# The lowest score level of a gated linear recurrence, from window products to folded dot products

## The chip, the cores and the metric

One NeuronCore of a Trainium2 chip runs the whole program. The metric is device time in microseconds; the time of a kernel is the median of several executions. The engines named below are TensorE (PE; PEld is its weight load), VectorE (DVE), ScalarE (ACT), GpSimd (POOL) and SyncE (SP, which only issues DMAs here).

## The reference

A trunk of two residual layers over 512 tokens of width 2048, all in float32. The first, mixer A, is a gated linear recurrence (HGRN2) with 16 heads of 128 features; the second, mixer B, is softmax attention with forget gates. What matters here is mixer A's score matrix. For each head, with q and k of shape (512, 128) and g the log of the forget gate,

```python
b = jnp.cumsum(gc, axis=-2)
diff = b[..., :, None, :] - b[..., None, :, :]
decay = jnp.exp(jnp.where(mask, diff, -jnp.inf))
A = jnp.einsum('bhtd,bhsd,bhtsd->bhts', qc, kc, decay)
```

so a score A[t, s], s <= t, is the sum over the 128 features of q[t] k[s] times the product of the forget gates between s and t, and the output is A v, then a norm by head, a SiLU gate and the output projection.

## The kernel before

**Data.** Everything lies transposed: 128 features on the partitions, the 512 tokens along the free axis (T = 512, P = 128), in four windows of 128 tokens (NW = 4). Products are made in float32r with each factor split into a high and a low part: `split(src, h, l)` (L443) casts on ScalarE (L444) and takes the difference on VectorE (L445), and a product is three matmuls, high by high, high by low, low by high. `sum_parts` (L332) sums over the 128 partitions in another way: VectorE adds the upper 64 partitions to the lower 64 (L337), the sum's high part is cast into the lower half of a tile (L338) and its low part written to the upper half (L339), and one matmul with the constant matrix `ones` sums all 128 rows and puts the sum on every row (L340).

**Groups and tasks.** The projections run in groups (`group`, L220): 16 k-steps of twelve 512-column matmuls (L238 to L244), with the weights loaded by DMA and split just ahead (three buffers each of `wh` and `wl`). Mixer A has 16 groups in a hand-written order, `order_a` (q0 v0 q1 q2 v1 q3 g0 ...). After each k-step `pump` (L91) advances the waiting heads' generators by `RATE_A` = 2 steps, so the heads' work is placed between the matmuls of the groups. A head's generator is `mix_a` (L610); each `yield` in it ends a step. With this order as its starting point, the framework plans the order of instructions on each engine from the costs and due times that it assumes for them.

**A head in mixer A.** The scores are built by levels into the tile `at` (128 source tokens on the partitions, by window and query token). The lowest level covers blocks of four tokens: query and key 0 to 3 tokens apart (d = 0, 1, 2, 3) in the same block. `e` holds the gates' products over 1, 2, 3 and 4 tokens. Before, the level splits k (`k_split`), makes `pr`, q times the gates for d = 1 to 3 (L632), splits q and `pr` into `mh` and `ml` (two windows at a time), and for each window multiplies k's 128 tokens by 320 columns (`win_scores`, L592 to L594); of this product only the few diagonals are wanted, which four `put_scores` for each window pick with masks (a predicated copy, L587). Then q and k are scaled by the gates (L644, L649) for the next level. Two more levels (m = 4, 16), a level of 64-token halves (copied into `at` at L733) and products between windows (with scalings at L747) follow; at last `at` is split window by window into `ah` and `al` (L760, with offsets `AOFF` = 0, 512, 1024, 896) and multiplied by v in `attend` (L429).

The functions as they were before the change:

## Time and profile before

| | |
|---|---|
| median of 3 runs | 2010.18 us (2009.14 to 2012.45) |
| the profiled execution's own time | 2011.1 us |
| its span in the trace | 2009.4 us, mean granted TensorE clock 0.995 |
| TensorE, weight loads | 1978.4 us (98%), 1695.3 us (84%) |
| VectorE, ScalarE, GpSimd | 1558.7 us (78%), 1130.1 us (56%), 207.3 us (10%) |
| mixer A's stretch | 0 to about 878 us of the span |
| HBM | 184.73 MB read, 96 GB/s over the span with the writes |

A row of a group of instructions reads: line, engine, operation, output<-inputs by the program's names, partitions x elements, count | busy time in us, mean ns of one | idle time of the engine before them, and what ended it. A matmul's duration contains its latency; what one costs in a stream is the distance from its start to the next one's. A row of a wait reads: who <- for whom, us in total, times, longest. A row of a window reads: the stretch and its length, busy time of PE, PEld, DVE, ACT and POOL, granted clock, DMA share, GB/s.

### The profile page before, as it was taken

The page shows a single profiled execution, that of the slowest core. Times are in us where ns is not written, and L with a number is a line of the kernel's source. Part 1 is how long each engine was busy: PE and PEld are TensorE (multiplying, and loading weights), DVE is VectorE, ACT ScalarE, POOL GpSimd, SP SyncE. Part 2 cuts the span into 40 slices and gives each one's busy share as a digit, 9 for nine tenths or more (in the row PEclk, how much of TensorE's full clock was granted, in tenths as well). Part 3 has the DMA queues.
Part 4 walks back from the last instruction along what each step waited for, and adds up shares of the span by engine and source line. Part 5 has one row for each costly group of instructions (what it writes and reads, how often), then busy time and mean ns, then how long its engine had stood idle before and what let it go on. Part 6 is the DMA issues. An engine that isn't in the chain of part 4 may idle for free.

```text
span 2009.4 us, 28900 instructions
## 1 busy us (share of the span) xinstructions
PE 1978.4 (98%) x10218; PEld 1695.3 (84%) x10218; DVE 1558.7 (78%) x3321; ACT 1130.1 (56%) x2311; POOL 207.3 (10%) x365
## 2 busy tenths in 40 slices
PE   9999999999999999989999999999999999999898
PEld 7888888888888888879987888888888888888898
DVE  7969987979798889797893677776766676687877
ACT  6646655657566466653464555665555556576332
POOL 3303110203122030010000000000000000000100
PEclk9999999999999999999999999999999999999999
DMA  5222222222222222243432222322223332323443
GB/s 190 74 88 81 74 84 74 84 78 80 83 76 74 74 84 84 84 155 120 157 118 95 95 87 87 95 90 94 85 89 90 94 95 90 90 84 106 137 157 105
DMA packets 57600, 195.01 MB, mean 97 GB/s; under 512 B 7904, under 2 KB 8032, under 8 KB 57456
## 3 DMA queue, kind: packets, MB, share of 16 engines
q1 hardware_dynamic: 52192, 176.39, 28.0%
q0 software_dynamic: 5120, 16.78, 2.5%
q8 instruction: 80, 1.31, 0.3%
q14 instruction: 64, 0.52, 0.1%
q10 hardware_dynamic: 144, 0.01, 0.0%
HBM read 184.73 MB, written 8.42 MB: 96 GB/s over the span
## 4 chain that ended last, share of the span: by engine, by line
PE 83%; DVE 7%; DMA 5%; issue 3%; ACT 1%; POOL 1%; SPq 0%; POOLq 0%; DVEq 0%; ACTq 0%
PE gm L244 17%; PE gm L242 17%; PE gm L243 17%; PE gm L238 6%; PE gm L240 6%; PE gm L239 6%; DMA wr<-in_wa_q 3%; DVE w7l L445 2%; PE mx L594 2%; PE mx L593 2%; PE mx L592 1%; DMA wr<-in_wb_q 1%; PE mx L439 1%; PE mx L440 1%; PE mx L438 1%
## 5 line engine op out<-in xcount | busy, mean ns | idle before, releaser
L242 PE MATMUL gm<-xh,wh 128*128 128x512 f32 x1664 | 650.5, 392 | 0.1
L243 PE MATMUL gm<-xl,wh 128*128 128x512 f32 x1664 | 650.2, 391 | 0.0
L244 PE MATMUL gm<-xh,wl 128*128 128x512 f32 x1664 | 610.8, 392 | 0.2 <-DVE wl L445 0.2
L243 PEld LDWEIGHTS gm<-xl,wh 128*128 128x128 f32 x1664 | 313.2, 188 | 62.8
L242 PEld LDWEIGHTS gm<-xh,wh 128*128 128x128 f32 x1664 | 313.3, 188 | 62.6 <-DVE z L390 0.3
L244 PEld LDWEIGHTS gm<-xh,wl 128*128 128x128 f32 x1664 | 312.0, 188 | 62.6 <-DVE wl L445 0.9
L444 ACT CAST wh<-wr 128x512 fp32r<-128x512 f32 x288 | 177.3, 621 | 155.2 <-PE gm L243 112.7
L445 DVE TENSOR_TENSOR wl<-wr,wh 128x512 fp32r<-128x512 f32 x288 | 204.8, 714 | 67.2 <-ACT wh L444 57.3
L147 ACT ACTIVATE wh<-wr,v_b_norm_w 128x256 fp32r<-128x256 f32 (+1 forms) x192 | 111.6, 584 | 187.1 <-PE gm L243 152.1
L148 DVE SCALAR_TENSOR_TENSOR wl<-wr,v_b_norm_w,wh 128x256 fp32r<-128x256 f32 (+1 forms) x192 | 109.3, 570 | 131.6 <-ACT wh L147 126.4
L239 PE MATMUL gm<-wl,xh 128*128 128x512 f32 x512 | 200.2, 392 | 0.0
L240 PE MATMUL gm<-wh,xl 128*128 128x512 f32 x512 | 199.3, 392 | 0.0
L238 PE MATMUL gm<-wh,xh 128*128 128x512 f32 x512 | 179.6, 393 | 2.4 <-DVE q L556 1.6
L147 ACT ACTIVATE wh<-wr,v_kv_norm_w 128x256 fp32r<-128x256 f32 (+1 forms) x192 | 110.0, 573 | 56.1 <-PE gm L240 44.1
L148 DVE SCALAR_TENSOR_TENSOR wl<-wr,v_kv_norm_w,wh 128x256 fp32r<-128x256 f32 (+1 forms) x192 | 109.2, 570 | 32.7 <-ACT wh L147 32.1
L587 DVE COPY_PREDICATED at<-masks,mx 128x128 f32<-128x128 uint8 (+4 forms) x448 | 108.4, 296 | 13.6 <-PE mx L594 13.2
L238 PEld LDWEIGHTS gm<-wh,xh 128*128 128x128 f32 x512 | 95.8, 188 | 22.1 <-DVE q L556 1.9
L240 PEld LDWEIGHTS gm<-wh,xl 128*128 128x128 f32 x512 | 96.2, 188 | 19.0
L239 PEld LDWEIGHTS gm<-wl,xh 128*128 128x128 f32 x512 | 96.3, 188 | 18.8
L953 POOL TENSOR_SCALAR_AFFINE_SELECT s<-s 128x128 f32<-128x128 f32 x64 | 28.4, 444 | 741.6 <-DVE s L952 741.1
L444 ACT CAST w7h<-wr 128x768 fp32r<-128x768 f32 x48 | 40.1, 835 | 114.5 <-PE mx L297 48.8
L444 ACT CAST kh<-k 128x512 fp32r<-128x512 f32 (+1 forms) x96 | 56.4, 587 | 44.2 <-PE mx L593 19.0
(232 smaller groups left out, 3879.8 us busy)
## 6 DMA issues: line engine op xcount, KB each, us to landing
wr<-in_wb_qk SPq DMA_DIRECT2D x64, 512.0 KB, 3.5
wr<-in_wa_qf SPq DMA_DIRECT2D x62, 512.0 KB, 3.5
wr<-in_wa_v SPq DMA_DIRECT2D x32, 512.0 KB, 3.5
wr<-in_wa_g SPq DMA_DIRECT2D x32, 512.0 KB, 3.5
wr<-in_wb_v SPq DMA_DIRECT2D x32, 512.0 KB, 3.6
wr<-in_wb_g SPq DMA_DIRECT2D x32, 512.0 KB, 3.5
wr<-in_wa_q SPq DMA_DIRECT2D x24, 512.0 KB, 3.5
wr<-in_wb_q SPq DMA_DIRECT2D x24, 512.0 KB, 3.6
```

The costliest lines, as they stand in the source:

```text
L147: S.activation(h[:, c], r[:, c], AF.Copy, scale=w[:, kt : kt + 1])
L148: V.scalar_tensor_tensor(l[:, c], r[:, c], w[:, kt : kt + 1], rd(h)[:, c], op0=ALU.mult, op1=ALU.subtract)
L238: PE.matmul(banks[j], xh, h, start=f, stop=False)
L239: PE.matmul(banks[j], xh, l, start=False, stop=False)
L240: PE.matmul(banks[j], xl, h, start=False, stop=e)
L242: PE.matmul(banks[j], h[:, c], Xh[kt], start=f, stop=False)
L243: PE.matmul(banks[j], h[:, c], Xl[kt], start=False, stop=False)
L244: PE.matmul(banks[j], l[:, c], Xh[kt], start=False, stop=e)
L444: S.copy(h, src)
L445: return V.tensor_sub(l, src, rd(h))
L587: V.copy_predicated(out, mv, data)
L593: PE.matmul(lv[:, base : base + n], kh[:, c], ml, start=False, stop=False)
```

## The change

It has four parts, all in mixer A.

1. The lowest level makes dot products elementwise. `p0` = q k (d = 0) and `pr` = q times gates times the k of d tokens before (d = 1, 2, 3, with 384, 256 and 128 columns) lie feature by feature on the partitions; `half_parts` folds the upper 64 partitions onto the lower and stacks high and low parts of the 64 sums, as `sum_parts` does; three matmuls with `ones` (512, 512 and 256 columns) give each token's score on every partition, and one `put_scores` for each d, over all four windows, picks the wanted place. k isn't split at this level, and a head has two steps fewer.
2. In mixer A `sum_parts` casts on ScalarE in place of VectorE.
3. The copies of the half level into `at` and the three scalings of q between windows go from VectorE to ScalarE.
4. The split of `at` is made by one pair of instructions for three windows and one for the fourth, in place of four pairs.

```diff
--- before.py
+++ after.py
@@ -79,6 +79,7 @@
             cur["ctx"].close()
         cur["ctx"] = c = ExitStack()
         cur["t"] = 3 if name[0] == "o" else 4
+        cur["name"] = name
         cur["sb"] = c.enter_context(tc.tile_pool(name=f"sb{name}", bufs=1, reuse_waits="tile"))
 
     phase("a")
@@ -335,9 +336,16 @@
         s = x
         hl = mt("sl", (P, T), 2, F32R)
         V.tensor_add(s[:half], x[:half], x[half:])
-        V.tensor_copy(hl[:half], s[:half])
+        (S.copy if cur["name"] == "a" else V.tensor_copy)(hl[:half], s[:half])
         V.tensor_sub(hl[half:], s[:half], rd(hl)[:half])
         PE.matmul(out_bank, ones, hl, start=True, stop=True)
+
+    def half_parts(x, hl):
+
+        half = P // 2
+        V.tensor_add(x[:half], x[:half], x[half:])
+        S.copy(hl[:half], x[:half])
+        V.tensor_sub(hl[half:], x[:half], rd(hl)[:half])
 
     def rsqrt_mean(out, sums, n):
         S.activation(out, sums, AF.Ln, scale=1.0 / n, bias=eps)
@@ -625,40 +633,33 @@
         reached.add(("g", h))
         yield
 
-        kh, kl = k_split(h, k)
-        pr = mt("pr", (P, NW, 192), 1)
-        for d, c0 in ((1, 0), (2, 96), (3, 160)):
+
+        p0 = rd(mt("kl", (P, T), 2, F32R))
+        pr = mt("pr", (P, 768), 1)
+        V.tensor_mul(p0, q, k)
+        for d, c0 in ((1, 0), (3, 384), (2, 512)):
             n = 4 - d
-            V.tensor_mul(
-                view(pr, c0, [[192, NW], [n, 32], [1, n]]),
-                view(q, d, [[P, NW], [4, 32], [1, n]]),
-                view(e, (d - 1) * T + d, [[P, NW], [4, 32], [1, n]]),
-            )
+            o = view(pr, c0, [[n, P], [1, n]])
+            V.tensor_mul(o, view(q, d, [[4, P], [1, n]]), view(e, (d - 1) * T + d, [[4, P], [1, n]]))
+            V.tensor_mul(o, o, view(k, 0, [[4, P], [1, n]]))
         yield
-        for w0 in (0, 2):
-            mh, ml = m_tiles(h)
-            for dst, src, step, n in ((0, q, P, P), (P, pr, 192, 192)):
-                d = [[320, 2], [1, n]]
-                split(view(src, w0 * step, [[step, 2], [1, n]]), view(mh, dst, d), view(ml, dst, d))
-            if w0:
-                V.tensor_mul(
-                    view(q, 0, [[4, P], [1, 4]]),
-                    view(q, 0, [[4, P], [1, 4]]),
-                    view(e, 0, [[4, P], [T + 1, 4]]),
-                )
-                V.tensor_mul(
-                    view(k, 0, [[4, P], [1, 3]]),
-                    view(k, 0, [[4, P], [1, 3]]),
-                    view(e, 2 * T + 3, [[4, P], [-T, 3]]),
-                )
+        hl, hl0 = m_tiles(h)
+        half_parts(p0, hl0[:, :T])
+        half_parts(pr, hl)
+        V.tensor_mul(view(q, 0, [[4, P], [1, 4]]), view(q, 0, [[4, P], [1, 4]]), view(e, 0, [[4, P], [T + 1, 4]]))
+        kv = view(k, 0, [[4, P], [1, 3]])
+        V.tensor_mul(kv, kv, view(e, 2 * T + 3, [[4, P], [-T, 3]]))
+        yield
+        for x, w, parts in (
+            (hl0, T, ((0, 0),)),
+            (hl, T, ((1, 0), (3, 384))),
+            (hl[:, T:], 256, ((2, 0),)),
+        ):
+            lv = lv_bank()
+            PE.matmul(lv[:, :w], ones, x[:, :w], start=True, stop=True)
+            for d, c0 in parts:
+                put_scores(at, lv, 0, NW, c0, (4 - d) * 32, 1, d, d)
             yield
-            for i in range(2):
-                lv = lv_bank()
-                c = slice(i * 320, (i + 1) * 320)
-                win_scores(lv, 0, w0 + i, kh, kl, mh[:, c], ml[:, c], 320)
-                for d, c0 in ((0, 0), (1, P), (2, P + 96), (3, P + 160)):
-                    put_scores(at, lv, w0 + i, 1, c0, T, 1, d, d)
-                yield
 
         n = P
         tt = t1
@@ -730,7 +731,7 @@
             c = slice(w * P, (w + 1) * P)
             win_scores(lv, w * P, w, kh, kl, mh[:, c], ml[:, c], P)
         for i in range(2):
-            V.tensor_copy(
+            S.copy(
                 view(at, i * P + 64, [[2 * P, 2], [1, 64]])[0:64],
                 view(lv, i * 64, [[P, 2], [1, 64]])[i * 64 : (i + 1) * 64],
             )
@@ -744,9 +745,7 @@
         split(q[:, 3 * P :], mh[:, 640:768], ml[:, 640:768])
         pr = mt("pr", (P, 3, P), 1)
         for i, (w, j) in enumerate(((2, 1), (3, 3), (3, 2))):
-            V.tensor_scalar(
-                out=pr[:, i, :], in0=q[:, w * P : (w + 1) * P], scalar1=ew[:, j : j + 1], scalar2=None, op0=ALU.mult
-            )
+            S.activation(pr[:, i, :], q[:, w * P : (w + 1) * P], AF.Copy, scale=ew[:, j : j + 1])
         split(pr[:, 0:2, :].rearrange("p a c -> p (a c)"), mh[:, 128:384], ml[:, 128:384])
         split(pr[:, 2, :], mh[:, 512:640], ml[:, 512:640])
         reached.update((("qk", h), ("half", h)))
@@ -755,9 +754,9 @@
             yield
         ah = mt("ah", (P, 1280), 1, F32R)
         al = mt("al", (P, 1280), 1, F32R)
-        for w in range(NW):
-            c = slice(AOFF[w], AOFF[w] + P)
-            split(at[:, w, :], ah[:, c], al[:, c])
+        d = [[T, 3], [1, P]]
+        split(at[:, 0:3, :], view(ah, 0, d), view(al, 0, d))
+        split(at[:, 3, :], ah[:, AOFF[3] : AOFF[3] + P], al[:, AOFF[3] : AOFF[3] + P])
         for part in (((0, 0, 384), (2, 384, 128)), ((1, 0, 256),)):
             lv = lv_bank()
             for w, base, n in part:
```

## The prediction

> **What bounds the kernel now.** I read the page first for the busiest engine and the chain, then the windows by stage, then TensorE's waits, and only then the operations that the change touches.

> ```profile
> PE 1978.4 (98%) x10218; PEld 1695.3 (84%) x10218; DVE 1558.7 (78%) x3321; ACT 1130.1 (56%) x2311; POOL 207.3 (10%) x365
> ...
> PE 83%; DVE 7%; DMA 5%; issue 3%; ACT 1%; POOL 1%; SPq 0%; POOLq 0%; DVEq 0%; ACTq 0%
> ```

> TensorE works in 98% of the span and holds 83% of the chain that ended last. Mixer A runs up to about 878 us; the windows (busy us of PE, weight loads, DVE, ACT, POOL, then clock) give that stretch by itself:

> ```profile
> 0.00:878.00 878.00, 873.03 (x4243) 738.72 (x4244) 746.68 (x1779) 542.64 (x1176) 146.32 (x241) 1.00 0.28 88
> ```

> 873 of 878 us of TensorE are taken. VectorE stands at 746.7/878 = 85% and ScalarE at 542.6/878 = 62%. So VectorE is full enough to matter, though not the bound. TensorE's waits in the same stretch, of which the largest inside the loop are these two:

> ```profile
> PE gm L238 <- DVE q L556: 1.6, 2, 1.1
> PE mx L592 <- ACT mh L444: 0.9, 3, 0.6
> ```

> Columns: us in total, times, longest. 2.5 us in some 850: whatever the other engines do, TensorE hardly notices. In this stretch the time is therefore what TensorE has to execute, and matmuls taken out of its queue should come off the end one for one.

> **The change, part by part.**

> *The lowest level on TensorE.* Before, each of the 16 heads runs four windows of three 320-column products:

> ```profile
> L594 PE MATMUL mx<-mh,kl 128*128 128x320 f32 x64 | 19.5, 309 | 0.0
> L593 PE MATMUL mx<-ml,kh 128*128 128x320 f32 x64 | 19.5, 308 | 0.0
> L592 PE MATMUL mx<-mh,kh 128*128 128x320 f32 x64 | 17.1, 307 | 0.0
> ```

> That is 192 matmuls. Their 308 ns are latency, since they overlap; what one costs is the distance from start to start, which the timeline has (start us, us, engine, line):

> ```profile
> 463.53 0.31 PE L593 MATMUL mx<-ml,kh 128*128 128x320 f32 x1
> ...
> 464.70 0.39 PE L239 MATMUL gm<-wl,xh 128*128 128x512 f32 x1
> ```

> Eight 320-column products start between these two rows: 1.17/8 = 146 ns each. Removed: 192 x 0.146 = 28.0 us. Added are, for each head, products of the constant ones matrix with 512, 512 and 256 columns. The same 512-column product exists in the norm sums, and 256-column ones in the quick products:

> ```profile
> 448.66 0.40 PE L340 MATMUL mx<-sl,ones 128*128 128x512 f32 x1
> 448.90 0.39 PE L238 MATMUL gm<-wh,xh 128*128 128x512 f32 x1
> ```
> ```profile
> 929.75 0.28 PE L298 MATMUL gm<-xh,w7l 128*128 128x256 f32 x1
> ...
> 930.95 0.28 PE L296 MATMUL gm<-xh,w7h 128*128 128x256 f32 x1
> ```

> 448.66 to 448.90 is 0.24 us; 929.75 to 930.95 holds ten at 0.12 us. Added: 16 x (0.24 + 0.24 + 0.12) = 9.6 us. Net: 28.0 - 9.6 = 18.4 us less on the path. [...]

> *VectorE.* The rows of mixer A (busy us, mean ns of one):

> ```profile
> L445 DVE TENSOR_TENSOR kl<-k,kh 128x512 fp32r<-128x512 f32 x64 | 45.7, 715 | 4.6 <-ACT kh L444 4.6
> L445 DVE TENSOR_TENSOR ml<-pr,mh 128x384 fp32r<-128x384 f32 x64 | 38.8, 613 | 0.5 <-ACT mh L444 0.5
> L587 DVE COPY_PREDICATED at<-masks,mx 128x128 f32<-128x128 uint8 x128 | 36.2, 296 | 11.5 <-PE mx L594 11.4
> L445 DVE TENSOR_TENSOR ml<-q,mh 128x256 fp32r<-128x256 f32 x64 | 26.5, 415 | 0.0
> L587 DVE COPY_PREDICATED at<-masks,mx 128x192 f32<-128x192 uint8 x64 | 22.7, 369 | 1.8 <-PE mx L594 1.8
> L445 DVE TENSOR_TENSOR al<-at,ah 128x128 fp32r<-128x128 f32 x64 | 14.9, 281 | 0.1
> L632 DVE TENSOR_TENSOR pr<-q,e 128x384 f32<-128x384 f32 x16 | 13.2, 825 | 0.4 <-ACT e L621 0.4
> L337 DVE TENSOR_TENSOR t<-t 64x512 f32<-64x512 f32 x16 | 11.2, 698 | 11.8 <-ACT t L404 11.6
> L747 DVE TENSOR_SCALAR pr<-q,ew 128x128 f32<-128x128 f32 x48 | 11.1, 278 | 0.1
> L394 DVE TENSOR_TENSOR z<-z,t 128x512 f32<-128x512 f32 x16 | 10.8, 683 | 0.0
> L445 DVE TENSOR_TENSOR tl<-wm,th 128x768 fp32r<-128x768 f32 x2 | 1.8, 952 | 0.0
> ```

> Out, for each head: one split of k (0.715), two of q (0.83) and two of pr (1.23), sixteen predicated copies, one for each window and offset, at the 0.296 of the 128-column form (4.7), and four al differences replaced by one of 384 columns and one of 128 (1.12 - 0.61 - 0.28 = 0.23): 7.7 us. In: q times k over 512 columns, as L394 (0.68); three further products of pr with k, taken like the three of L632 and in proportion to their columns (0.825 x 6/3 = 1.65); the two folds, each an addition of the upper to the lower 64 partitions and a difference, as L337 for 512 columns (2 x 0.70) and as the 768-column row for the other (2 x 0.95), since the row's length and not the partitions count (64x512 at 698, 128x512 at 683): 3.3; four predicated copies over all windows, 512, 384, 256 and 128 columns wide, on the line through 296 and 369 ns, 1.14 ns a column: 0.73 + 0.59 + 0.44 + 0.30 = 2.1. In all 7.7 us: the level itself is even for VectorE. What relieves it is the moves: three scalings (0.83) go to ScalarE, and the cast of the norm sum and two copies of scores with them. At least 16 x 0.83 = 13 us less, so 733 us in a stretch of 859: 85%, as before. All of it lies beside matmuls; the price if that cover went is the slower case below.

> *ScalarE.* Its rows:

> ```profile
> L444 ACT CAST wh<-wr 128x512 fp32r<-128x512 f32 x269 | 165.5, 621 | 147.3 <-PE gm L243 110.9 <-PE gm L240 14.9 <-DMA wr<-in_wa_qf 13.2
> L444 ACT CAST kh<-k 128x512 fp32r<-128x512 f32 x64 | 39.9, 623 | 33.0 <-PE mx L593 15.1 <-DVE k L720 12.0 <-PE mx L594 2.0
> L444 ACT CAST mh<-pr 128x384 fp32r<-128x384 f32 x64 | 32.7, 520 | 11.4 <-DVE pr L632 7.4 <-DVE pr L683 3.9
> L444 ACT CAST mh<-q 128x256 fp32r<-128x256 f32 x64 | 25.9, 409 | 17.6 <-DVE q L696 9.0 <-DVE q L556 3.5 <-DVE q L719 2.7
> L444 ACT CAST ah<-at 128x128 fp32r<-128x128 f32 x64 | 14.9, 302 | 15.7 <-DVE at L733 15.5
> L444 ACT CAST th<-wm 128x768 fp32r<-128x768 f32 x2 | 1.6, 829 | 0.0
> ```

> Out: 0.62 + 2 x 0.41 + 2 x 0.52 + (4 x 0.302 - 0.52 - 0.30) = 2.9 us a head. In: casts of 512 and 768 columns (0.62 + 0.83), the norm sum's cast (0.62), and five 128-column pieces, three scalings and two copies, at 0.302 each (1.5): 3.6 us. So 0.7 x 16 = 11 us more, 554 of 859 us, 64%. The first row says how much room the weights have: ScalarE stood 110.9 us idle ahead of a weight cast because TensorE had not yet freed a buffer. It casts ahead of need, so some tenths of a microsecond more in its queue hide there.

> *Waits added.* The fold is a chain VectorE, ScalarE, VectorE, TensorE: the cast waits on ScalarE for the addition, with the weight casts queued behind it, and the second difference waits for the cast. The norm sum has lived with that chain (L337 to L340) without a TensorE wait on it, and a cast at 0.62 in place of VectorE's only lengthens it by about 0.2 us. That shows where TensorE waits for the first norm (L556, the 1.6 us row): +0.2 us, at most 0.4. DMAs, SP's and POOL's queues gain and lose nothing, and POOL's sums still run beside the other heads; the number of steps a head yields falls by two, which lets the heads of a pair end some four steps earlier in groups that have steps to spare.

> **Sum.** Against the profiled execution (span 2009.4 us, its own time 2011.1) 18.4 - 0.2 = 18.2 us less, so 1992.9 for such an execution; it lies 0.9 us over the median of 2010.18, and the median becomes 1992.0.

> The two waits can vanish (-2.5). Below that there is the clock: at the handover to the output product the windows show

> ```profile
> 898.00:905.00 7.00, 3.91 (x18) 3.91 (x19) 5.35 (x9) 1.99 (x2) 0.46 (x1) 0.51 0.95 359
> ```

> a granted clock of 0.51 with 3.91 us of work, worth up to 2 us if an earlier arrival there escapes it, and as much again at the same handover of mixer B. That gives 1992 - 6 = 1986 as the low end.

> **The rivals.**

> *New waits, still a gain.* The instruction order of every engine is planned from assumed costs; another mix gives another order. The two waits above are what such mismatches cost now. The folds put two dependent crossings between VectorE and ScalarE in front of matmuls where the old level had one; half a microsecond of waiting a head, as the longest at L592 (0.6), is 8 us: 2000.

> *VectorE's burst makes it slower.* The products (0.68 + 1.65 + 1.65 = 4.0 us) and the folds (3.3) now fall into two consecutive steps, the second with q's and k's scalings that the old level had too, and one k-step of a group, twelve matmuls of at most 0.24 us = 2.9 us, releases two steps. If the weight differences (wl) queue behind, TensorE lacks weights for up to 7.3 - 2.9 = 4.4 us, 16 times 70 us. It decides from 18.2/16 = 1.14 us a head; with half the 4.4, 35 us are lost: 2027. For it speaks VectorE's 85%. Against it: a gate evacuation already puts three operations like L394 for each of four banks on VectorE at once, 8.2 us, and in the whole stretch TensorE's waits for VectorE inside the loop come to under 2 us.

> *TensorE isn't the limit.* If its 98% were an artefact of overlapping records, the time would follow VectorE at 85%, whose load changes by 13 us in 747: 2010 to 1998, and 2010 if the relief lies where it is idle. [...] The start distances speak against it: successive matmuls begin without a gap beyond their columns.

> *More than the sum.* If VectorE's relief is larger than bounded, and both handovers keep full clock with a shorter wait: below 1986.

> **How the numbers follow.** The main case, 1986 to 1998, has 0.72; new waits (around 2000) 0.12; no limit on TensorE (2010) 0.04; the burst (2027) 0.06; more than the sum (near 1983) 0.06. The range 1986 to 2002 leaves out the last three and a third of the second: it holds about 0.8. The three runs of before spread over 3.3 us, 0.16%, so 0.2% or 4 us is about what can be told from no change. Faster 0.90, same 0.04, slower 0.06.

> **What would show it.** Right: the 320-column rows of L592 to L594 are gone; the new ones products start about 0.23 and 0.12 us apart; mixer A's TensorE busy time falls from 873 to about 855 us and its end from 878 to about 859; TensorE's waits in it stay under 5 us; VectorE's busy time falls by 13 us or more and ScalarE's rises by about 11. Wrong: waits of TensorE on the new folds or on wl, VectorE near full in the stretch, or a clock below 1.00 within mixer A.

## The result, and the profile after

The change made the kernel slower: 2036.28 us (median of 4, 2033.83 to 2037.63) against 2010.38 us, a ratio of 1.0129 with a 95% interval of 1.0114 to 1.0144. The forecast was 1992, 1986 to 2002. The profiled execution has a span of 2035.8 us.

The page of the changed kernel, engines and chain:

```profile
PE 1976.4 (97%) x10074; PEld 1681.2 (83%) x10074; DVE 1581.7 (78%) x3048; ACT 1146.0 (56%) x2328; POOL 203.6 (10%) x365
...
PE 65%; DVE 11%; DMA 4%; issue 4%; ACT 2%; POOL 0%; POOLq 0%; DVEq 0%; ACTq 0%
```

The 144 matmuls are gone from the count (10218 to 10074), yet TensorE is busy for only 2 us less, and its share of the chain fell from 83% to 65%. Where mixer A ends I take from the first matmul of the output product's first group, the 3073rd of the 512-column group products: 849.5 us before, 878.5 us now, 29.0 us later; what follows takes 1157 us now and 1160 before. So all of the loss lies in mixer A. (The 878 us of the kernel before, in the sections above, lie 28.5 us inside the output product's first group; that the number comes back here is chance.) The two windows up to those ends, before and then after (stretch, length, busy us of PE, weight loads, DVE, ACT, POOL, then the granted clock):

```profile
0.00:849.50 849.50, 844.53 (x4118) 715.11 (x4119) 721.21 (x1730) 523.31 (x1141) 143.98 (x237) 1.00 0.28 86
```
```profile
0.00:878.50 878.50, 843.72 (x3974) 700.79 (x3975) 743.93 (x1456) 540.03 (x1157) 140.46 (x237) 0.98 0.27 83
```

Three things are read there. TensorE stands idle for 878.5 - 843.7 = 34.8 us, before for 5.0. VectorE's busy time rose by 22.7 us, where 13 or more should have come off, though its share of the stretch is still 85%. And the granted clock is no longer 1.00. TensorE's waits in the stretch, the largest:

```profile
PE mx L600 <- ACT mh L452: 7.7, 5, 4.0
PE mx L600 <- DVE at L595: 6.0, 5, 2.7
PE mx L659 <- DVE mh L348: 4.2, 2, 2.3
PE gm L243 <- ACT v L433: 4.0, 3, 2.7
PE gm L239 <- DVE q L564: 3.0, 2, 2.0
PE gm L245 <- DVE wl L453: 3.0, 3, 1.8
```

They are spread over everything that VectorE feeds, itself or through ScalarE: the next level's products (L600), the new ones products (L659), the evacuations, the weights. No single new wait stands out. What VectorE does ahead of one of them, the 2.7 us in which L600 waits until 381.09 us for a bank that mask copies (L595) hold, the timeline shows:

```profile
363.28 0.73 DVE L595 COPY_PREDICATED at<-masks,mx 128x512 f32<-128x512 uint8 x1
...
374.42 1.16 DVE L453 TENSOR_TENSOR wl<-wr,wh 128x512 fp32r<-128x512 f32 x1
375.50 0.55 DVE L697 TENSOR_TENSOR q<-q,t 128x384 f32<-128x384 f32 x1
...
378.53 0.73 DVE L595 COPY_PREDICATED at<-masks,mx 128x384 f32<-128x384 uint8 x1
379.12 0.67 DVE L453 TENSOR_TENSOR kl<-k,kh 128x512 fp32r<-128x512 f32 x1
379.71 0.60 DVE L453 TENSOR_TENSOR ml<-q,mh 128x384 fp32r<-128x384 f32 x1
380.23 0.71 DVE L595 COPY_PREDICATED at<-masks,mx 128x128 f32<-128x128 uint8 x1
```

VectorE runs from 359 to 384 us without a pause. The second mask copy starts 15 us after the first; the last of those listed ends at 380.94 us, and TensorE, idle for 2.65 us by then, starts its next product at 381.09.

Nearly all pauses of TensorE come after such a stretch, which the mean of 85% hides. From 20 us on, TensorE pauses 27 times in the changed kernel's mixer A (gaps over 0.15 us); in 26 of these cases VectorE had no such gap in the 10 us up to the moment when TensorE went on. The kernel before has full stretches too: cut into pieces of 10 us, VectorE is over 97% busy in 32 of its first 84 and under 80% in 26. Two of them (the third busy time is VectorE's):

```profile
300.00:310.00 10.00, 10.00 (x49) 8.49 (x48) 6.01 (x17) 4.18 (x8) 0.00 (x0) 1.00 0.19 54
360.00:370.00 10.00, 10.00 (x57) 8.76 (x55) 10.00 (x30) 6.21 (x14) 7.31 (x11) 1.00 0.22 81
```

VectorE's idle time, 128 us before and 135 after, lies in other places, the largest part of it ahead of weight differences that wait for ScalarE's casts (54.9 us before, 61.2 after, from 5 us on).

The half-clock stretches show in windows laid on the clock's changes (the first three of seven):

```profile
106.70:110.10 3.40, 3.40 (x12) 2.92 (x11) 3.26 (x8) 3.40 (x13) 0.00 (x0) 0.50 0.51 157
219.40:222.80 3.40, 3.40 (x9) 2.63 (x8) 3.40 (x8) 3.19 (x7) 0.10 (x1) 0.51 0.37 146
383.20:386.60 3.40, 3.40 (x12) 2.92 (x11) 3.40 (x7) 0.41 (x1) 0.10 (x1) 0.50 0.39 149
```

TensorE is busy for all of these 3.4 us, but its 512-column products start 0.43 us apart in such a stretch (at 776.02, 776.45 and 776.88 us, for example) and 0.227 us at full clock. There are six of 3.4 us and one of 6.8, 27.3 us in all, each near a pause of 1.8 us or more. TensorE works in 25.1 us of them, so half speed costs some 12.5 us. The trace shows what goes ahead of them: all seven start a whole number of steps of 3.41 us after the first, and in the step just ahead TensorE was idle for 53 to 82% (from 5 us on, no other step at full clock in mixer A was over 49% idle). The steps ahead of the first and the third:

```profile
103.29:106.70 3.41, 1.49 (x8) 0.98 (x7) 3.31 (x6) 3.31 (x9) 0.00 (x0) 1.00 0.35 139
379.79:383.20 3.41, 0.95 (x4) 0.73 (x5) 3.41 (x8) 1.78 (x6) 1.34 (x4) 1.00 0.15 10
```

The account of the 29.0 us: -18.4 of matmuls, +29.8 of pauses, +12.5 of half clock, which is 23.9. Of the other 5.1 an estimated 3.4 is what the accounting of a pause leaves out, since a matmul ahead of one is counted with its full latency (0.39 in place of 0.227 us, 28 pauses where there were 7); the last 1.7 stays unexplained.

### The profile page after: what moved, and what is told of

Same layout as the page of the kernel before. It is cut to its first block, busy times and chain, and to the rows that moved or that the text cites. A ratio compares the mean times of both kernels' runs of the same rounds, so it can differ in the third digit from the quotient of the medians.

```text
span 2035.8 us, 28275 instructions
## 1 busy us (share of the span) xinstructions
PE 1976.4 (97%) x10074; PEld 1681.2 (83%) x10074; DVE 1581.7 (78%) x3048; ACT 1146.0 (56%) x2328; POOL 203.6 (10%) x365
## 4 chain that ended last, share of the span: by engine, by line
PE 65%; DVE 11%; DMA 4%; issue 4%; ACT 2%; POOL 0%; POOLq 0%; DVEq 0%; ACTq 0%
PE gm L243 15%; PE gm L244 14%; PE gm L245 14%; PE gm L239 3%; PE gm L240 3%; PE gm L241 3%; DMA wr<-in_wb_q 3%; DVE w7l L453 2%; DVE wl L453 2%; DMA wr<-in_wa_q 1%; PE mx L968 1%; PE mx L447 1%; PE mx L448 1%; PE mx L446 1%; PE mx L602 1%
## 5 line engine op out<-in xcount | busy, mean ns | idle before, releaser
L243 PE MATMUL gm<-xh,wh 128*128 128x512 f32 x1664 | 654.8, 394 | 5.2 <-ACT v L433 4.0
L243 PEld LDWEIGHTS gm<-xh,wh 128*128 128x128 f32 x1664 | 315.3, 190 | 71.8 <-ACT v L433 5.6
L240 PE MATMUL gm<-wl,xh 128*128 128x512 f32 x512 | 201.9, 395 | 0.5 <-DVE wl L453 0.3
L239 PE MATMUL gm<-wh,xh 128*128 128x512 f32 x512 | 179.7, 396 | 3.8 <-DVE q L564 3.0
L149 DVE SCALAR_TENSOR_TENSOR wl<-wr,v_kv_norm_w,wh 128x256 fp32r<-128x256 f32 (+1 forms) x192 | 109.2, 570 | 32.7 <-ACT wh L148 32.1
L239 PEld LDWEIGHTS gm<-wh,xh 128*128 128x128 f32 x512 | 96.9, 190 | 24.7 <-DVE q L564 3.5
L240 PEld LDWEIGHTS gm<-wl,xh 128*128 128x128 f32 x512 | 96.9, 189 | 20.4 <-DVE wl L453 1.8
L241 PEld LDWEIGHTS gm<-wh,xl 128*128 128x128 f32 x512 | 96.9, 189 | 19.5
L452 ACT CAST w7h<-wr 128x768 fp32r<-128x768 f32 x48 | 40.1, 835 | 116.1 <-PE mx L298 54.9
L595 DVE COPY_PREDICATED at<-masks,mx 128x192 f32<-128x192 uint8 (+5 forms) x256 | 97.4, 404 | 10.1 <-PE mx L659 4.7
L452 ACT CAST ah<-mx 128x384 fp32r<-128x384 f32 (+2 forms) x128 | 46.3, 371 | 45.9 <-PE mx L968 19.9
```

Source lines behind the costliest of these rows:

```text
L149: V.scalar_tensor_tensor(l[:, c], r[:, c], w[:, kt : kt + 1], rd(h)[:, c], op0=ALU.mult, op1=ALU.subtract)
L239: PE.matmul(banks[j], xh, h, start=f, stop=False)
L240: PE.matmul(banks[j], xh, l, start=False, stop=False)
L241: PE.matmul(banks[j], xl, h, start=False, stop=e)
L243: PE.matmul(banks[j], h[:, c], Xh[kt], start=f, stop=False)
L452: S.copy(h, src)
```

## The experiments

Each time is a median of four or more runs; the ratio is to the kernel before on the same chip. "VectorE" is its busy time up to the end of mixer A, "lost" TensorE's pauses plus half of its half-clock time there (a pause inside a half-clock stretch counts one and a half times, which makes at most 2 us). These last three columns are of the profiled execution; in e4 it took 2017.8 us, 4 us more than the median, in the others it lies within 3 us of it.

| run | us | ratio, 95% interval | mixer A's end | VectorE | lost |
|---|---|---|---|---|---|
| before | 2010.4 | | 849.5 | 721 | 3 |
| after | 2036.3 | 1.0129 [1.0114, 1.0144] | 878.5 | 744 | 46 |
| e1_level_only | 2046.9 | 1.0181 [1.0162, 1.0199] | 884.7 | 767 | 50 |
| e2_moves_only | 2008.6 | 0.9992 [0.9982, 1.0002] | 847.5 | 697 | 2 |
| e3_seven_steps | 2020.0 | 1.0046 [1.0031, 1.0061] | 860.3 | 742 | 26 |
| e4_no_pool_sums | 2013.6 | 1.0018 [1.0008, 1.0029] | 858.5 | 716 | 31 |
| e5_rate | 2017.9 | 1.0038 [1.0023, 1.0053] | 860.0 | 741 | 26 |
| e6_seven_rate | 2020.6 | 1.0053 [1.0038, 1.0068] | 859.5 | 740 | 26 |
| e7_scale_first | 2035.7 | 1.0123 [1.0106, 1.0140] | 876.2 | 738 | 44 |
| e8_before_more_vector | 2038.1 | 1.0136 [1.0121, 1.0151] | 876.8 | 755 | 26 |
| e9_less_vector | 2019.6 | 1.0043 [1.0028, 1.0058] | 858.7 | 722 | 27 |
| e10_no_folds | 2018.5 | 1.0041 [1.0026, 1.0056] | 855.1 | 709 | 13 |
| e11_no_folds_seven | 2024.0 | 1.0068 [1.0046, 1.0089] | 859.8 | 708 | 18 |
| g1_no_folds_rate | 2017.6 | 1.0029 [1.0017, 1.0041] | 852.3 | 712 | 11 |
| g2_less_vector_seven | 2025.1 | 1.0065 [1.0050, 1.0080] | 864.2 | 724 | 31 |
| g3_no_folds_less | 2014.4 | 1.0010 [1.0001, 1.0020] | 849.2 | 691 | 10 |
| g4_before_spread | 2053.3 | 1.0203 [1.0186, 1.0220] | 891.0 | 755 | 43 |
| h1_products_gpsimd | 2028.3 | 1.0088 [1.0072, 1.0105] | 864.9 | 701 | 20 |
| h2_banks_early | 2031.5 | 1.0105 [1.0090, 1.0120] | 871.5 | 712 | 30 |

**Which part of the change.** First the level alone, with parts 2 to 4 undone:

> Only the lowest level is changed; the casts, copies, scalings and the split of at stand as before. Level theory (VectorE's work of the new level comes later than its place in TensorE's order allows): TensorE's gaps in mixer A stay near the 33 us of the changed kernel, and with them the half-clock windows; 2030 to 2045 us. Moves theory (ScalarE's queue, with more casts that wait on VectorE, is what comes late): the gaps go and the 18 us of removed matmuls show; 1990 to 1998 us.

2046.9 us, worse than the whole change. Then those parts alone, on the old level:

> Only the moves to ScalarE and the merged split of at; the lowest level stands as before. Level theory: VectorE has 13 us less or more, TensorE has what it had, so 2006 to 2012 us and gaps of 2 to 4 us. Moves theory: gaps of 15 us or more in mixer A, some half-clock windows, 2025 us or more.

2008.6 us, no difference that counts. The level is the cause; the moves to ScalarE help by some 11 us on top of it (2046.9 to 2036.3) and hardly at all without it. The windows of the two runs say why that is plausible:

```profile
0.00:884.70 884.70, 844.24 (x3973) 701.54 (x3974) 766.62 (x1586) 511.38 (x1092) 141.54 (x237) 0.99 0.26 83
```
```profile
0.00:847.50 847.50, 843.80 (x4118) 714.65 (x4119) 697.08 (x1601) 548.37 (x1206) 141.19 (x237) 1.00 0.28 86
```

The level alone adds 45 us to VectorE (721.2 to 766.6); the moves take 24 off. With TensorE full, 24 us less on VectorE bring 2 us.

**Is it VectorE's load by itself?** The kernel before, with reductions added that nothing reads and no matmul removed:

```diff
+        junk = mt("junk", (P, 1), 2)
+        for i in range(2):
+            V.tensor_reduce(out=junk, in_=k, axis=AX.X, op=ALU.max, negate=True)
         yield
+        for i in range(2):
+            V.tensor_reduce(out=junk, in_=k, axis=AX.X, op=ALU.max, negate=True)
         for w0 in (0, 2):
```

> The kernel before with four reductions of k to a column that nothing reads, two in each of the two steps ahead of the lowest level's products: 4 x 0.68 = 2.7 us of VectorE's time for each head, as much as the new level adds (45 us in all), and no TensorE work removed. Density theory: gaps of 15 us or more in mixer A and half-clock windows, 2025 us or more. Chain theory: nothing hangs on the reductions, so 2010 to 2015 us.

```profile
L639 DVE TENSOR_REDUCE junk<-k 128x1 f32<-128x512 f32 x32 | 21.7, 679 | 1.9 <-ACT k L569 1.4
L642 DVE TENSOR_REDUCE junk<-k 128x1 f32<-128x512 f32 x32 | 21.7, 677 | 0.2
```
```profile
PE mx L592 <- DVE at L587: 4.3, 4, 1.5
PE mx L593 <- DVE ml L445: 2.7, 4, 1.3
PE mx L592 <- ACT mh L444: 2.4, 2, 2.2
PE gm L244 <- DVE wl L445: 2.3, 3, 1.1
```

43.4 us of idle work on VectorE, and the old kernel is 27.7 us slower, with the same scattered waits as the changed one (second fence: TensorE's waits). This is the clearest of the runs: most of the added work could not be hidden, although TensorE had waited for VectorE for hardly 2 us and VectorE stands idle for 122 us even here. That idle time is not where the work falls: counted as above, VectorE was again without a gap for 10 us in 21 of TensorE's 23 pauses. The run isn't a pure test of load, though: the framework planned a new order for it. TensorE's 4117 products run in the order of the kernel before for the first 288 and in another from there on, so the 27.7 us are those of the load together with the order that came with it. The same reductions at other places, one in each product step of the middle levels:

```diff
             for w0 in (0, 2):
+                junk = mt("junk", (P, 1), 2)
+                V.tensor_reduce(out=junk, in_=k, axis=AX.X, op=ALU.max, negate=True)
                 lv = lv_bank()
```

> The kernel before with the same four reductions for each head (43 us of VectorE's time), one in each of the four product steps of the two middle levels in place of two and two ahead of the lowest. Load theory: as slow as there, 2030 to 2040 us. Burst theory: single operations fit in, 2012 to 2024 us.

2053.3 us: almost the whole 43 us, and worse than bunched. So the theory that operations released together are the harm, and single ones fit in, fell; where the load stands moves the time by some 15 us, but not in the way that I thought. Counted as above, 12 of its 17 pauses follow 10 us of VectorE without a gap; the other 5, two of them of over 3.6 us, do not, so here the load alone doesn't explain them.

**Spreading the level.** Two more step ends in the changed kernel, and then a slower release of steps:

```diff
         V.tensor_mul(p0, q, k)
+        yield
...
         half_parts(p0, hl0[:, :T])
+        yield
         half_parts(pr, hl)
```

> The changed kernel with two more step ends in the lowest level (after q times k, and between the two folds), so that a head has as many steps as before. If the burst is a matter of how many operations one step releases: fewer gaps in mixer A, half or less of the 33 us, below 2020 us. If the order that the planner makes doesn't hang on the step ends, or the level is late for another reason: 2030 us or more.

```diff
-RATE_A, RATE_B = 2, 1
+RATE_A, RATE_B = 1.5, 1
```

> The changed kernel with RATE_A 1.5 in place of 2: a k-step of a group releases one and a half steps of the heads, so a pair's work spreads over 26 or 27 of a group pair's 32 k-steps and not 20. Density theory (VectorE gets more in a stretch than it can do in it): gaps in mixer A fall from 33 to 15 us or less, few half-clock windows, below 2010 us. Chain theory (each head's way through the new level is too long for the places of its matmuls, whenever they come): gaps stay at 25 us or more, 2025 us or more.

Either takes 16 to 18 us off, 2020.0 and 2017.9 us, mostly half-clock time (27.3 us to 3.4 in both); the pauses fall far less than either density or burst theory asked (26 us of idle TensorE are left in both). Together:

> RATE_A 1.5 and the two more step ends of the run with seven steps (2020 us there). Density theory: the two add up, gaps under 10 us, 1993 to 2003 us. Chain theory: no better than the seven steps alone, 2015 to 2025 us.

2020.6 us: they do not add up, which speaks against a simple density in time. With q's and k's scalings put ahead of the folds:

> The changed kernel with q's and k's scalings ahead of the folds in place of behind them, so that the next level's chain starts 3.3 us of VectorE's work earlier, at the same load. Chain theory: the waits of the next level's first product (L600 for mh and for at, 14 us) fall to half, below 2026 us. Density theory: the same load in the same stretch, the waits move to the folds' products; within 6 us of 2036.

2035.7 us: the chain to the next level isn't what is long; the waits changed places.

**Taking load off the changed kernel.** GpSimd's first two sums of gates left out:

```diff
-        G.tensor_add(e[:, 1, 1:], g[:, 1:], g[:, :-1])
-        G.tensor_add(e[:, 2, 2:], e[:, 1, 2:], g[:, :-2])
...
-        S.activation(e[:, 1, 1:], e[:, 1, 1:], AF.Exp)
+        S.activation(e[:, 1, 1:], g[:, 1:], AF.Exp)
```

> The changed kernel with two of GpSimd's three sums of gates left out (the exponentials read g itself, so the gates over two and three tokens are wrong), 42 us of GpSimd's busy time. If VectorE is late because operations with two inputs in SBUF stand still while GpSimd reads (the 64x768 difference at 1140 in place of 950 ns): VectorE's busy time in mixer A falls by 10 us or more, gaps halve, below 2022 us. If that isn't what makes it late: within 5 us of 2036.

2013.6 us, and VectorE lost 28 us though nothing was taken from it. Some of its operations are shorter (first the changed kernel, then this one):

```profile
L348 DVE TENSOR_TENSOR mh<-pr,mh 64x768 fp32r<-64x768 f32 x16 | 18.2, 1140 | 0.5
```
```profile
L348 DVE TENSOR_TENSOR mh<-pr,mh 64x768 fp32r<-64x768 f32 x16 | 15.4, 959 | 0.5
```

The changed kernel's own trace shows where the longer ones lie. Of its 16 differences of this form nine overlap with no operation of GpSimd and take 944 to 953 ns. Seven overlap with its sums of gates: four of them, each beside two sums, take 1678 to 1731 ns; the other three take 952 to 954, and there it is the sum that is long, 1.80 us, the longest three of its 16 (1.04 us the shortest). The run isn't pure, though: without the sums a head's gates are also ready earlier. Next the products of pr with k left out (`V.tensor_mul(o, o, view(k, ...))` deleted):

> The changed kernel with the three products of pr with k left out (the scores at distance 1 to 3 in a block lack their k), about 20 us of VectorE's time in mixer A, all else the same. Density theory: VectorE falls to about 722 us, what it had before, gaps in mixer A fall from 33 to 10 us or less, and most of TensorE's saving shows: 1993 to 2005 us. If VectorE's amount isn't what counts: 2025 us or more.

2019.6 us at 722 us of VectorE, between what the two theories gave: with the load that VectorE had before the change, 27 us are lost where the old level loses 3. The folds replaced by products of both parts:

```diff
-        half_parts(p0, hl0[:, :T])
-        half_parts(pr, hl)
+        split(p0, xh0[:, :T], xl0[:, :T])
+        split(pr, xh, xl)
...
-            PE.matmul(lv[:, :w], ones, x[:, :w], start=True, stop=True)
+            PE.matmul(lv[:, :w], ones, x[:, :w], start=True, stop=False)
+            PE.matmul(lv[:, :w], ones, y[:, :w], start=False, stop=True)
```

> The changed kernel without the folds: both parts of all 128 partitions are kept, and the ones products run twice, on the high and on the low part (96 ones products in place of 48). VectorE loses the two additions over half the partitions, 26 us; TensorE pays 9.6 us more, so it has 9 us less than before the change. Density theory: VectorE at 718 us or less, gaps of 10 us or less, 1999 to 2010 us. If the folds' load isn't what counts: 2036 + 10 us.

2018.5 us: VectorE fell to 709 us, no half clock, 13 us lost; half of what the load theory hoped for. With the step ends:

> The same without folds, with two more step ends (after q times k, and between the two splits). Density theory: as without folds or some us below, 1998 to 2006 us. If the step ends count by themselves, as the 16 us between 2036 and 2020 suggested: 5 us or more below the run without folds.

2024.0 us, so no gain; a loss isn't certain, as the four times (2018.9 to 2028.2) overlap those of the run without step ends (2016.8 to 2022.0). The slower release on it, and the step ends on the run without products:

> Without folds (2018 us) and RATE_A 1.5. If what is left there is the burst of operations released together: gaps from 12 to 6 us or less, 2005 to 2012 us. If it is the level's own chain (bank, mask copies, next level): within 4 us of 2018.

> The products of pr with k left out (2020 us) and the two more step ends. Burst theory: the step ends take some 14 us here as they took 16 from the changed kernel, 2003 to 2009 us. Load alone: VectorE is at 722 us as there, so within 4 us of 2020.

2017.6 and 2025.1 us: the slower release brings nothing more without folds, and step ends, worth 16 us on the changed kernel, cost 5 on the one without products. Both reliefs in one, no folds and no products:

> Without folds and with the products of pr with k left out (scores at distance 1 to 3 lack their k): VectorE near 689 us, 33 below the kernel before, with the level's steps and waits as they are. Load theory: gaps of 4 us or less, TensorE's 9 us less show whole, 1999 to 2003 us. If the level itself is late whatever the load: gaps of 8 us or more, 2008 us or more.

2014.4 us. VectorE stands 30 us below the kernel before, mixer A ends where it did before, and TensorE still loses 10 us.

**The rest.** Two tries at it. ScalarE copies the level's three banks to SBUF, so that the mask copies hold none:

```diff
+            S.copy(p0 if y is xl0 else y[:, :w], lv[:, :w])
+            s = p0 if y is xl0 else rd(y)[:, :w]
             for d, c0 in parts:
-                put_scores(at, lv, 0, NW, c0, (4 - d) * 32, 1, d, d)
+                put_scores(at, s, 0, NW, c0, (4 - d) * 32, 1, d, d)
```

> Without folds (2018 us), and each of the three banks of the level copied to SBUF by ScalarE (24 us of it in all, scores at distance 1 to 3 rounded to the matmul's input format), the mask copies reading there. If the wait of L600 for the mask copies is one for a free bank: it goes (5 us to 1 or less), 2008 to 2013 us. If it is VectorE's load that shows there: the wait moves elsewhere, within 4 us of 2018.

L600's wait for the mask copies fell from 5.1 to 1.7 us as for a bank, but other waits more than took its place: 2031.5 us. And q k and the products with k on GpSimd (`G.tensor_mul`):

> Without folds, and q times k and the three products of pr with k on GpSimd in place of VectorE (28 us off VectorE, some 50 us onto GpSimd). Load theory without contention: as without the products, 2011 to 2016 us. If GpSimd's reading of SBUF holds VectorE up, as the run without its sums suggested (23 us for 42 us of GpSimd): VectorE's busy time falls by 15 us or less and the time is 2020 us or more.

2028.3 us: VectorE's busy time fell by 8 us of the 28 moved, and operations that were not touched grew longer, as those beside GpSimd's sums had in the changed kernel (L575 from 695 to 926 ns, the split of k from 745 to 822). GpSimd was busy for 91 us more and not some 50, and VectorE waited 16.7 us for its products, so the run doesn't show how much of its time the lengthening costs.

## Why the prediction was wrong

*Right: the matmuls.* In the changed trace the 512- and 256-column ones products start 0.234 and 0.120 us before their successors (medians), and the 320-column rows are gone. So the 18.4 us, counted from start to start, did come off TensorE's work.

*Wrong, the deciding step: "whatever the other engines do, TensorE hardly notices".* That was concluded from 2.5 us of waits and 85% on VectorE. Few waits say that VectorE keeps up at this load; they don't say how much more it could carry. In the two load runs, each with the order planned for it, it was little or nothing: 43 us more cost 28 or 42 us. The mean misled, because VectorE was already full in some two fifths of the 10 us pieces. Nor can TensorE's saving show in a stretch where VectorE works without a pause: shortening TensorE's queue leaves VectorE the same work in less time.

*Wrong, a term of the sum: VectorE's load.* "The level itself is even for VectorE" measured +45 us (in the run with the level alone), and the whole change, priced at 13 us less or better, measured +22.7. The largest error is in the mask copies. Of before and after, the rows of the page and the new ones by shape:

```profile
L587 DVE COPY_PREDICATED at<-masks,mx 128x128 f32<-128x128 uint8 (+4 forms) x448 | 108.4, 296 | 13.6 <-PE mx L594 13.2
```
```profile
L595 DVE COPY_PREDICATED at<-masks,mx 128x192 f32<-128x192 uint8 (+5 forms) x256 | 97.4, 404 | 10.1 <-PE mx L659 4.7
```
```profile
L595 DVE COPY_PREDICATED at<-masks,mx 128x256 f32<-128x256 uint8 x16 | 11.8, 736 | 3.0 <-PE mx L659 2.4 <-DVE at L595 0.5
L595 DVE COPY_PREDICATED at<-masks,mx 128x512 f32<-128x512 uint8 x16 | 11.8, 735 | 2.5 <-PE mx L659 2.3
L595 DVE COPY_PREDICATED at<-masks,mx 128x384 f32<-128x384 uint8 x16 | 11.7, 733 | 0.4
```

I took 256 copies at 0.296 us out and 64 at 0.30 to 0.73 in, 42 us less; the busy time fell by 11, so this term accounts for 31 of the 45 us. The old copies overlapped, 108.4/448 = 0.24 us each and not 0.296, and the new ones take 0.73 us whether they write 256, 384 or 512 columns, so there was no price by the column. For TensorE I had counted from start to start, for VectorE durations. The folds came out near their estimate: 0.95 and 0.69 us for the additions, 1.14 and 0.69 for the differences, 3.5 us and not 3.3.

*The rival came true in size, for another reason.* VectorE's burst was priced at 2027 and given 0.06; the evidence set against it was that 8.2 us of evacuation were absorbed at once. The runs bear the burst out in part at most: spreading the level's operations took 16 to 18 us off the changed kernel, but on the old kernel single reductions did more harm than bunched ones. That the measured time lies near 2027 owes something to luck: the price came from half of an assumed lack of weights of 4.4 us a head, while TensorE's waits for weight differences were 3.3 us in all.

*Missing: the clock.* Pauses were priced at their length. Seven half-clock stretches came with them and cost some 12.5 us, over two fifths of the whole loss. The prediction names "a clock below 1.00 within mixer A" as a sign of being wrong, but put it into no rival's price.

*What stays open.* At lower VectorE load than before (709 and 691 us) the new level still loses 10 to 13 us where the old one loses 3, and step ends or a slower release move the time by anything from 18 us down to 5 us up. The amount of work is thus not all of it. At 691 us VectorE is still over 97% busy in 31 of the 84 pieces of 10 us, against 32 before the change, so its total went down and its full stretches stayed. That the planned order fits some mixes of work better than others is likely, but no run here holds the order fixed, so it is argued and not shown. The load runs leave it open too, since TensorE's order changed in both (after the first 288 products, and after 348 with the reductions in the middle levels). No version beat both kernels clearly; the moves alone, 2008.6 us, are within the noise.

## What to carry to other kernels

An engine at 85% beside a full one, with nobody waiting for it, may still be at its limit in part of the time: look at its busy time in short pieces and not only at the mean, and before trading work from the full engine to it, load it with work that nothing reads and see whether the time moves (and whether a planner changed the order meanwhile). Cost instructions by what they add to their engine's busy time (busy divided by count, or start to start), not by their mean duration, on every engine alike. A pause of TensorE of some 2 us was paid for nearly twice here where the clock fell with it (3.4 us at half speed cost some 1.6 us more, estimated from the 0.43 and 0.227 us above).
